# Attention and linear attention of a decoder block as small steps in an order fixed by the source

## The chip, the cores and the metric

The kernel runs as one program on one core of a Trainium2 chip. A core has a matrix engine (TensorE, PE), a vector engine (VectorE, DVE), an engine for activation functions (ScalarE, ACT), a general engine (GpSimd, POOL) and an engine that here only issues transfers (SyncE, SP). Each engine runs its own list of instructions in order and waits for the others by semaphores. The metric is the device time of one execution in microseconds (us). Each kernel is timed several times and the median counts; one execution is also taken apart by the hardware profiler.

## The reference

One decoder block over 512 tokens (T, in four blocks of P = 128) of width 1024. A mixer of two parallel parts, attention in a window of 128 with sinks and gated linear attention, is followed by a retrieval of 16 experts out of 16384 in each of 8 heads. A vector c scales, shifts and gates both (six modulations).

```python
h = rms_norm(x, norm1_w) * (1.0 + scale1) + shift1
proj = h @ w_in            # aq, ak, av, gq, gk, gv, gg, glr
scores = einsum('bnqhgd,bnkhd->bnhgqk', qb, kb) * 64 ** -0.5      # 8 heads, 2 of keys, width 64
probs = softmax(concatenate([where(mask, scores, -inf), sink], -1))[..., :-1]
att = einsum('bnhgqk,bnkhd->bnqhgd', probs, vb)

def step(state, inp):                                   # per head: 4 heads, keys 64, values 128
    b = cumsum(log_a); inter = (q * exp(b)) @ state
    decay = exp(b[t] - b[s])                            # for s <= t
    att = sum_d(q[t, d] * k[s, d] * decay[t, s, d]); intra = att @ v
    state = exp(b_last) * state + (k * exp(b_last - b)).T @ v
    return inter + intra
go = rms_norm(go, gla_norm_w) * silu(gg)
x = x + gate1 * (concatenate([att, go]) @ w_out)

h2 = rms_norm(x, norm2_w) * (1.0 + scale2) + shift2
x = x + gate2 * peer_ffn(h2, ...)                       # product keys, top 16, gather of u and v rows
return rms_norm(x, final_norm_w)
```

## The kernel before

**Precision.** Weights and activations are split into a high and a low part (`hi`, `lo`), and a product takes three matmuls: high by high, low by high, high by low (`mm3`, L78 to L80). The split is a copy on ScalarE and a subtraction on VectorE.

**Stages.** First come the norm, four modulations and the projections to q, k and the decays (up to L667). Then the stage that is changed, L677 to L892. Then the mixers (L907: the product of both parts with `w_out`, called `pw` in the trace, gate and second norm), the retrieval (first matmul `pq`) and the gathers and products of the experts, which take most of the time.

**The changed stage** has these works:
- `wide_part(g, ...)`: the projections to gv (g = 0) and gg (g = 1), 512 wide, in pairs of token blocks. Each pair takes two PSUM tiles `pn` and 8 steps of k with 6 matmuls. `wide_load(g)` brings `w_v` in two halves into the three `raw` tiles, and splits them.
- `attention(n)`, n = 0 to 3: for each half of the heads (jj) the mask and scores go into two banks `sc` (L723, L728), then maximum, Exp with sums (L739), Exp of the sink (L741), division by the sum (four scalings on VectorE, L745), transposes `pt` (L754), a copy `PT` (L755), the product with v into `po` (L760), and a copy into `mixA` (L763). Block 0 has one block of keys, the others two.
- `prep_*(1)` for the second 256 tokens: a scan of the decays, differences at NL levels, Abs (L332) and Exp (L335) over all levels in one pass each, products with q and k (the product q*k on GpSimd). The tile `Eg` holds them and is shared with gg.
- `gla_scores(n)`: decays by levels, 36 small matmuls and more into `pa` (a tile of two banks, `sc2`), the diagonal `pd` for two blocks each, merging under masks.
- `gla_state(n, gated)`: output `go` from state and scores (bank `po`), transposed keys `pk` and the new state's product `pS` (bank `pt`), four updates of the state S, then squares, root, and the scaling of `go`: for blocks 2 and 3 with gg in the same instruction, for 0 and 1 without; these get gg in `gla_gate`.
- `gla_gate(n)`: transposes `gt`, and the split of both parts for the mixers (`ah`, `al`, `gh`, `gl`).
- `mod_part(3)` and `(4)`: `w_ada` in four loads each through the same `raw` tiles, 8 sums on VectorE (L240), then 8 matmuls with one column (`mt`, L231).

**PSUM.** The eight banks are: `m` two (scores, `pd`, `mt`), `pt` one, `po` one, `sc2` two, `ph` two (`pn`, `gt`, later `pq`).

**The order.** Up to L667 the source fixes the order on each engine (`manual_schedule`). From L677 on, through the mixers, a planner orders the instructions by a simulated timeline:

```python
TCARGS = dict(schedule_with_timeline_sim=True)
```

Its input is the program text below; instructions that are ready early are moved ahead, on all engines and on SP's queue too. In the order that results, half of the 192 `pw` matmuls stand among the last steps of attention and of the states, and ScalarE's Silu of gg follows a load of its table.

```python
    gla_scores(0); attention(0); gla_scores(1)
    prep_scan(1); prep_diffs(1); prep_ends(1); prep_abs(1); prep_exp(1); prep_mults(1)
    wide_part(0, gv, (0, 1)); attention(1); wide_part(0, gv, (2, 3))
    gla_scores(2); gla_state(0, False); attention(2); gla_scores(3); gla_state(1, False)
    wide_part(1, gg, (0, 1)); attention(3); wide_part(1, gg, (2, 3))
    mod_part(3, ...); mod_part(4, ...)        # then Silu of gg, gg * gla_norm_w
    gla_state(2, True); gla_state(3, True)    # later gla_gate(0..3), mixers(0), mixers(2)
```

## Time and profile before

| | |
|---|---|
| three runs | 1457.5, 1461.05, 1461.68 us, median 1461.05 |
| profiled execution | 1457.49 us, of which the span is 1455.6 |
| TensorE busy | 1408.2 us, 97% |
| VectorE busy | 1274.2 us, 88% |
| ScalarE busy | 664.1 us, 46% |
| GpSimd busy | 611.8 us, 42% |
| transfers | 443.81 MB, 305 GB/s in the mean |

The span goes from the first instruction to the last; the profiled execution's own time is 1.9 us longer. Busy shares are means over stages with different limits: TensorE at 97% says that it is almost always at work, not that its work takes as little time as it could. The granted clock of TensorE tells how fast it was allowed to run. In a row of the timeline stand the start, the duration, the engine, the line, the operation, what it writes and reads, the shape and the number of instructions that were grouped; in brackets the idle time ahead and what ended it. A duration on TensorE is that of one matmul with its fill and drain; how much it costs in a stream is read from the distance between starts.

### The profile page before, as it was taken

The numbers are of one execution on the slowest core, as the hardware profiler recorded it, in microseconds if no ns is written. First come the engines' busy times: TensorE is split into PE (matmuls) and PEld (weight loads), VectorE is DVE, ScalarE is ACT, GpSimd is POOL, SyncE is SP. The second block draws the span as 40 slices with busy tenths as digits, with TensorE's granted clock in tenths as the row PEclk, the third lists the DMA queues.
The fourth block names the chain that finished last, engine by engine and source line by source line (L and its number), as shares of the span: only waits on it lengthen the run. The fifth ranks groups of instructions, "written<-read, shape, count | busy, mean of one in ns | idle before, by whom it ended". The sixth has DMA issues, their size and how long they took to land.

```text
span 1455.6 us, 23288 instructions
## 1 busy us (share of the span) xinstructions
PE 1408.2 (97%) x8788; PEld 1240.0 (85%) x8788; DVE 1274.2 (88%) x2338; ACT 664.1 (46%) x1108; POOL 611.8 (42%) x401
## 2 busy tenths in 40 slices
PE   6998989999999999999999999999999999999997
PEld 4776777798899999999998888888888888888885
DVE  7777746769999999999987999999999899899996
ACT  4555555643344467666774323333333323333333
POOL 2000000044443634423034776777777676555510
PEclk9998979999999999999999999999999999999999
DMA  9633407434256989989889999999999999999962
GB/s 355 243 124 115 169 6 254 152 133 182 95 179 254 415 308 360 362 316 345 306 307 407 413 412 412 413 412 409 397 403 396 401 372 412 399 411 411 412 251 73
DMA packets 129985, 443.81 MB, mean 305 GB/s; under 512 B 11952, under 2 KB 48592, under 8 KB 109520
## 3 DMA queue, kind: packets, MB, share of 16 engines
q1 hardware_dynamic: 71136, 256.40, 46.6%
q0 software_dynamic: 47136, 171.99, 30.1%
q10 hardware_dynamic: 11600, 13.93, 2.7%
q8 instruction: 69, 1.13, 0.3%
q14 instruction: 44, 0.36, 0.1%
HBM read 399.71 MB, written 42.47 MB: 304 GB/s over the span
## 4 chain that ended last, share of the span: by engine, by line
PE 77%; DVE 9%; issue 5%; DMA 4%; ACT 2%; POOL 2%; ACTq 0%; SPq 0%; POOLq 0%; DVEq 0%
PE acc L78 12%; PE acc L80 12%; PE acc L79 12%; PE ph L78 8%; PE ph L80 8%; PE ph L79 8%; POOL spr L1322 2%; PE pg L1243 2%; DMA wa<-in_w_ada_dram 2%; PE pw L78 1%; PE pw L79 1%; PE pw L80 1%; DVE macc L240 1%; PE pj L473 1%; PE pn L78 1%
## 5 line engine op out<-in xcount | busy, mean ns | idle before, releaser
L78 PE MATMUL ph<-h2Th,his 128*128 128x320 f32 x1024 | 320.1, 313 | 2.4 <-ACT his L1687 1.9
L80 PE MATMUL ph<-h2Th,los 128*128 128x320 f32 x1024 | 316.3, 310 | 2.5 <-DVE los L1694 1.8
L79 PE MATMUL ph<-h2Tl,his 128*128 128x320 f32 x1024 | 316.0, 309 | 0.0
L1378 POOL DMA_INDIRECT gu<-in_u_dram,ix_u x128 | 217.2, 1697 | 148.1 <-DVE gu L1388 82.9
L1413 POOL DMA_INDIRECT gv<-in_vP_dram,ix_v x128 | 210.8, 1647 | 109.6 <-DVE gacc L1418 86.9
L78 PEld LDWEIGHTS ph<-h2Th,his 128*128 128x128 f32 x1024 | 193.0, 188 | 4.3 <-ACT his L1687 2.1
L80 PEld LDWEIGHTS ph<-h2Th,los 128*128 128x128 f32 x1024 | 192.7, 188 | 3.3 <-DVE los L1694 2.0
L79 PEld LDWEIGHTS ph<-h2Tl,his 128*128 128x128 f32 x1024 | 193.1, 189 | 0.8
L1322 POOL DMA_INDIRECT spr<-in_u_dram,spix x64 | 104.8, 1637 | 170.5 <-DVE spr L1328 128.4
L79 PE MATMUL acc<-los,Ah 128*128 128x512 f32 x432 | 168.1, 389 | 0.0
L80 PE MATMUL acc<-his,Al 128*128 128x512 f32 x432 | 168.1, 389 | 0.0
L78 PE MATMUL acc<-his,Ah 128*128 128x512 f32 x432 | 168.0, 389 | 0.0
L1418 DVE SCALAR_TENSOR_TENSOR gacc<-gv,hg,gacc 128x1024 f32<-128x1024 f32 x127 | 162.6, 1281 | 1.6 <-DMA gv<-in_vP_dram,ix_v 1.4
L1388 DVE SCALAR_TENSOR_TENSOR gu<-gu,h2n 128x1024 f32<-128x1024 f32 x128 | 155.7, 1220 | 5.3 <-DMA gu<-in_u_dram,ix_u 5.3
L78 PE MATMUL acc<-hi,Ah 128*128 128x512 f32 x336 | 131.3, 391 | 0.0
L80 PE MATMUL acc<-hi,Al 128*128 128x512 f32 x336 | 131.1, 390 | 0.0
L79 PE MATMUL acc<-lo,Ah 128*128 128x512 f32 x336 | 130.7, 389 | 0.0
L1690 ACT ACTIVATE Ah<-gr 128x768 fp32r<-128x768 f32 x64 | 53.5, 836 | 135.8 <-PE acc L79 128.5
L71 ACT ACTIVATE his<-u 128x1024 fp32r<-128x1024 f32 x86 | 90.5, 1054 | 21.2 <-PE ph L79 9.5
L72 DVE TENSOR_TENSOR los<-u,his 128x1024 fp32r<-128x1024 f32 x75 | 91.6, 1224 | 8.4 <-ACT his L71 8.4
L80 PEld LDWEIGHTS acc<-his,Al 128*128 128x128 f32 x432 | 81.1, 188 | 16.9
L78 PEld LDWEIGHTS acc<-his,Ah 128*128 128x128 f32 x432 | 81.1, 188 | 16.8
(684 smaller groups left out, 2921.8 us busy)
## 6 DMA issues: line engine op xcount, KB each, us to landing
u<-in_uT_dram SPq DMA_DIRECT2D x43, 1024.0 KB, 7.6
gr<-Gd SPq DMA_DIRECT2D x15, 1536.0 KB, 11.1
Gd<-gs SPq DMA_DIRECT2D x10, 2048.0 KB, 9.8
gsp<-ge ACTq DMA_DIRECT2D x40, 320.0 KB, 6.1
wa<-in_w_ada_dram SPq DMA_DIRECT2D x12, 1024.0 KB, 5.4
wo<-in_w_out_dram SPq DMA_DIRECT2D x8, 1024.0 KB, 6.4
wq<-in_wq_dram SPq DMA_DIRECT2D x8, 1024.0 KB, 5.9
gp<-gsp SPq DMA_DIRECT2D x22, 320.0 KB, 10.7
```

Of the source, the lines that this page charges most:

```text
L71: nc.scalar.activation(hi, src, AF.Copy)
L72: lo_eng.tensor_tensor(lo, src, hi, OP.subtract)
L78: nc.tensor.matmul(acc, lh, rh, start=start, stop=False)
L79: nc.tensor.matmul(acc, lh, rl, start=False, stop=False)
L80: return nc.tensor.matmul(acc, ll, rh, start=False, stop=stop)
L1243: nc.tensor.matmul(pt[:, i, :], o12[:, g, 0, :, r], o2[:, g, m, :, r], start=(m == 0), stop=(m == 2))
L1322: nc.gpsimd.indirect_dma_start(out=sp[m], out_offset=None, in_=a["u"], in_offset=bass.IndirectOffsetOnAxis(ap=sp["ix", i][:, j:j + 1], axi ...
L1378: nc.gpsimd.indirect_dma_start(out=ur, out_offset=None, in_=a["u"], in_offset=bass.IndirectOffsetOnAxis(ap=ix_u[:, s:s + 1], axis=0))
L1388: nc.vector.scalar_tensor_tensor(ur, ur, 1.0, h2n, op0=OP.mult, op1=OP.mult, accum_out=hid[:, s:s + 1])
L1413: nc.gpsimd.indirect_dma_start(out=vr, out_offset=None, in_=a["vP"], in_offset=bass.IndirectOffsetOnAxis(ap=ix_v[:, s:s + 1], axis=0))
L1418: nc.vector.scalar_tensor_tensor(gacc, vr, hg[:, s:s + 1], gacc, op0=OP.mult, op1=OP.add)
L1690: nc.scalar.activation(grp(Ah), A, AF.Copy)
```

## The change

The stage from L677 to L892 is rewritten as generators, which yield before each small piece of work on one engine. A yield (`need`) names the engine, an assumed duration in us, the tiles that the piece takes, the marks that must have been set, and an urgency. `Weave.run` plays the threads against each other with one clock per engine: among the pieces of the engine that could start first, within 0.3 us of one another, it takes the one of highest urgency, and emits its instructions. The stage stands in `manual_schedule`, so the order of emission is the order on each engine. The mixers behind it are still ordered by the planner.

Further edits in the same stage:
- Attention's scores alternate between the two halves of the rows (s within j), after both masks. Of the four scalings by the sum, two stay on VectorE (L829), two go to ScalarE as a Copy with scale (L833).
- The preparation of the second 256 tokens: Abs (L1058) and Exp (L1060) in two parts, levels 0 to 3 and the rest; the products follow each part; q*k is on VectorE and not on GpSimd.
- `go` and `pk` with `pS` share one `sc2` tile, the kind that the scores `pa` use too, and hold it until the norm's products are written; `po` is left to attention, whose two halves are threads of their own, the second after the first's product. The products of the norm carry the weight `gnw`; gg is no longer multiplied by it, and `gla_gate` always multiplies by gg.
- Attention's scores are paced: unit u starts only after a row of `pn` that is given by `PACE` and `PACE0`.
- The first two halves of `w_v` are fetched in the stage ahead. The loads of `w_ada` stand between and behind those of `w_v`.
- Silu comes after all four `pn` of gg, and its table is loaded once, then the old one back. All of `gla_gate` and the split of attention's output stand in the stage, ahead of the mixers.

```diff
@@
+class Weave:
+    HOP, SLACK = 0.12, 0.3
...
+    def run(self, threads):
+        live = [[t, next(t), 0.0, urge, None] for urge, ts in threads for t in ts]
+        while live:
+            able = []
+            for th in live:
+                eng, us, take, after, urge = th[1]
+                if any(x not in self.marks for x in after) or any(len(self.slots[k]) < n for k, n in take.items()):
+                    continue
+                ready = [th[2] - self.HOP * (eng == th[4])] + [self.marks[x] for x in after] + [self.slots[k][n - 1] for k, n in take.items()]
+                able.append((max(self.busy.get(eng, 0.0), max(ready) + self.HOP), len(able), eng, th, th[3] + urge))
+            first = min(able)
+            at, _, _, th, _ = max((x for x in able if x[2] == first[2] and x[0] <= first[0] + self.SLACK),
+                               key=lambda x: (x[4], -x[1]))
...
@@
+    weave = Weave({"m": 2, "pt": 1, "po": 1, "sc2": 1, "ph": 2, "raw": 3, "hi": 3, "h32": 4, "sS": 2, "PT": 2, "sm": 2, "m4": 2})
...
+    def pace(u):
+        r = min(PACE * u - PACE0, 31)
+        return ([("sc", u - 1)] if u else []) + ([("rows", r // 16, r // 8 % 2 * 2, r % 8)] if r > 0 else [])
+
+    def attention(n, jj):
...
+        yield need("PE", 0.45 * w, {"m": 2, "sm": 1}, pace(2 * n + jj))
...
         for h in order[:2]:
             nc.vector.tensor_scalar(sS[:, h, :], sS[:, h, :], Z[:, h:h + 1], None, op0=OP.mult)
+        mark(("Z", n, jj))
+        yield need("ACT", 0.4 + 0.42 * w)
+        for h in order[2:]:
+            nc.scalar.activation(sS[:, h, :], sS[:, h, :], AF.Copy, scale=Z[:, h:h + 1])
...
-    def gla_state(n, gated):
+    def gla_state(n):
...
-        go = bank(f"go{n}", "po")
+        two = bank2(f"go{n}")
+        go, pk = two[:, 0], two[:, 1]
...
-                nc.vector.tensor_scalar(gv[n][:, gsl], go[:, gsl], r4[:, h:h + 1], None, op0=OP.mult)
+            nc.vector.scalar_tensor_tensor(gv[n][:, gsl], go[:, gsl], y[:, h:h + 1], gnw, op0=OP.mult, op1=OP.mult)
+        two = go = pk = None
+        free("sc2")
...
+    def second_exps():
+        yield need("ACT", 0.5, {}, ["b1", ("Dpe", 0)])
+        nc.scalar.activation(Eg[:, NL + 1, :], preps["b"], AF.Exp, scale=1.0 / TAU)
+        mark("e1")
+        for L0, L1 in ((0, 4), (4, NL + 1)):
+            yield need("ACT", 1.8 if L0 == 0 else 1.4, {}, [("diff", L1 - 1)])
+            nc.scalar.activation(Eg[:, L0:min(L1, NL), :], Eg[:, L0:min(L1, NL), :], AF.Abs)
+            yield need("ACT", 1.8)
+            nc.scalar.activation(Eg[:, L0:L1, :], Eg[:, L0:L1, :], AF.Exp, scale=-1.0 / TAU)
+            mark(("E", L1 - 1))
...
+        weave.run([(2.0, [gla_scores(0, ([], [])), gla_scores(1, ([], []))]), (1.9, [wide_load(0), wide_load(1)]),
+                   (1.4, [gla_gate(n) for n in range(NT)]), (1.3, [gla_state(n) for n in range(NT)]),
+                   (1.2, [attention(n, jj) for n in range(NT) for jj in range(2)]),
+                   (1.1, [second_exps(), second_prep(), gla_scores(2, ready), gla_scores(3, ready)]),
+                   (1.0, [wide_all(0, gv)]), (0.8, [wide_all(1, gg, [("Spe", 2), ("Spe", 3)]), gates()]),
+                   (0.0, [modulation(3, [("w", 1, 7)]), modulation(4)]),
+                   (0.0, [attention_parts(n) for n in range(NT)])])
```

The order moves at many places; three show how. **TensorE, the scores of attention.** Before, one mask and the two products of one half of the rows (`sc`) stood between `pn` matmuls:

```order
L784 MATMUL pa_1301<-Eg 64x32 x6
L350 MATMUL pd_1355<-sel,Eg 128x2 x4
L723 LDWEIGHTS identb
L723 MATMUL sc_1412<-am,identb 128x512
L728 MATMUL sc_1412<-kT,qT 128x256 x2
L79 MATMUL pn_1645<-wv102l,hTh 128x512
```

After, both masks come first, and the products alternate, with steps of other heads between them:

```order
L798 LDWEIGHTS identb
L798 MATMUL sc_1285<-am,identb 128x512
L798 LDWEIGHTS identb
L798 MATMUL sc_1286<-am,identb 128x512
L859 MATMUL po_1259<-PT_1279,vN 64x128 x4
L804 MATMUL sc_1285<-kT,qT 128x256
L804 MATMUL sc_1286<-kT,qT 128x256
L842 MATMUL pt_1302<-ident,sS_1253 128x128 x4
L804 MATMUL sc_1285<-kT,qT 128x256
L804 MATMUL sc_1286<-kT,qT 128x256
```

The four products of a unit, which some units of before had already side by side, now always alternate between the two banks.

**ScalarE, around the second preparation.** Before, Abs (L332) and Exp (L335) took all their levels at once, with the evictions of `pn` (L708) between them and attention's copy `PT` (L755) behind:

```order
L741 ACTIVATE es_942<-es_942 128x4
L332 ACTIVATE Eg<-Eg 128x3584
L798 ACTIVATE at_175<-atc_179 64x4x64 x2
L708 ACTIVATE gv_109<-pn_1093 128x512
L708 ACTIVATE gv_110<-pn_1094 128x512
L335 ACTIVATE Eg<-Eg 128x4096
L755 ACTIVATE PT_959<-pt_960 128x512
```

After, the two parts of each (L1058, L1060) stand between single steps, and the new scalings (L833) are among these:

```order
L833 ACTIVATE sS_1079<-sS_1079,Z_1063 128x128 x2
L1058 ACTIVATE Eg<-Eg 128x2048
L848 ACTIVATE PT_1120<-pt_1106 128x512
L1060 ACTIVATE Eg<-Eg 128x2048
L867 ACTIVATE mixA_114<-po_1050 128x512
L774 ACTIVATE gv_109<-pn_897 128x512
L774 ACTIVATE gv_110<-pn_898 128x512
```

The copy `PT` and the evictions thus stand ahead of the second part, and not behind the whole.

**TensorE, the end of the stage.** Before, the last steps of attention and of the states lay among the `pw` matmuls of the mixers:

```order
L80 MATMUL pw_2072<-his,gl_2032 128x512
L760 MATMUL po_1696<-PT_1777,vN 64x128 x4
L754 MATMUL pt_1789<-ident,sS_1748 128x128 x4
L760 MATMUL po_1696<-PT_1788,vN 64x128 x4
L814 MATMUL pk_1925<-ident,kl_1046 128x128 x2
L809 MATMUL go_1916<-S_170,qe_1047 128x128
```

After, the last `pn` is followed by the sums over partitions (`mt`) and two transposes (`gt`), and then come all `pw`:

```order
L122 MATMUL pn_1813<-wv17h,hTl 128x512
L1080 MATMUL mt_1970<-ones,macc_1636 128x1 x8
L1080 MATMUL mt_1982<-ones,macc_999 128x1 x8
L990 MATMUL gt_1996<-ident,gv_109 128x128 x4
L990 MATMUL gt_2006<-ident,gv_110 128x128 x4
L120 MATMUL pw_2068<-his,ah_1290 128x512
```

All 192 `pw` matmuls of the mixers now lie behind the states.

## The prediction

> **What bounds the kernel now.** I read the page first, then the busy time of two stretches, then TensorE's rows in order of time through them, and last the rows of the engines that it waits for.

> ```profile
> span 1455.6 us, 23288 instructions
> PE   6998989999999999999999999999999999999997
> PEclk9998979999999999999999999999999999999999
> PE 77%; DVE 9%; issue 5%; DMA 4%; ACT 2%; POOL 2%; ACTq 0%; SPq 0%; POOLq 0%; DVEq 0%
> ```

> TensorE (PE) carries 77% of the chain that ended last, and after its start it is at 8 and its clock below 9 in two slices only, the fourth and the sixth. A slice is 36.4 us: these are 109 to 146 and 182 to 218 us, and both lie in the changed part. The two orders of TensorE agree up to the first `pn` matmul at 99.26 us and again from the first matmul of the retrieval stage (`pq`) at 274.38 us; on the other engines the last difference lies in the same stage. So what decides is the time between those two matmuls, 175.1 us now; all that comes later has the same order and shifts with it.

> ```profile
> 99.20:213.70 114.50, 104.55 (x798) 78.96 (x799) 75.20 (x194) 57.00 (x146) 1.34 (x1) 0.88 0.30 103
> 213.70:274.40 60.70, 58.73 (x309) 46.53 (x308) 46.23 (x91) 37.66 (x78) 0.00 (x0) 0.98 0.56 192
> ```

> Columns: stretch, its us, busy PE, PE weight loads, DVE, ACT, POOL, granted clock, DMA share, GB/s. In the first stretch VectorE is busy 66% and ScalarE 50%, and TensorE has 10 us idle and 12% of its clock missing. Its own rows show that the two belong together:

> ```profile
> 102.37 0.39 PE L78 MATMUL pn<-wv000h,hTh 128*128 128x512 f32 x1
> 102.60 0.39 PE L79 MATMUL pn<-wv000l,hTh 128*128 128x512 f32 x1
> ...
> 115.34 0.48 PE L754 MATMUL pt<-ident,sS 128*128 128x128 f32 x1 [3.26 <-DVE sS L745]
> ...
> 121.67 0.63 PE L79 MATMUL pn<-wv00l,hTh 128*128 128x512 f32 x1
> 122.10 0.63 PE L80 MATMUL pn<-wv00h,hTl 128*128 128x512 f32 x1
> ...
> 124.17 0.39 PE L79 MATMUL pn<-wv01l,hTh 128*128 128x512 f32 x1
> ...
> 130.87 0.79 PE L78 MATMUL pn<-wv000h,hTh 128*128 128x512 f32 x1 [2.66 <-ACT gv L708]
> ...
> 134.39 0.39 PE L80 MATMUL pn<-wv002h,hTl 128*128 128x512 f32 x1
> ...
> 199.27 1.12 PE L760 MATMUL po<-PT,vN 128*64 128x128 f32 x8 [3.44 <-ACT PT L755]
> ...
> 212.98 1.11 PE L754 MATMUL pt<-ident,sS 128*128 128x128 f32 x4 [0.59 <-DVE S L825]
> ...
> 216.25 0.39 PE L80 MATMUL pw<-his,al 128*128 128x512 f32 x1
> ...
> 231.08 0.66 PE L760 MATMUL po<-PT,vN 128*64 128x128 f32 x8 [0.75 <-ACT PT L755]
> ...
> 263.26 0.50 PE L78 MATMUL pw<-his,ah 128*128 128x512 f32 x1 [0.75 <-DVE mg L928]
> ```

> Three waits of 3.26, 2.66 and 3.44 us; after each, matmuls start 0.43 us apart and not 0.23, until 124.2, 134.4 and 216.2: 8.8, 3.5 and 17.0 us at half rate, of which 14.6 us are lost. With the shorter waits (0.59, 0.75, 0.75, and 0.33 in a row below) 11.8 us are idle. After the two of 0.75 the rate stays full: the `po` group at 231.08 takes 0.66 and not 1.12.

> **The work that stays.** The start-to-start times at full rate:

> ```profile
> 152.96 0.66 PE L754 MATMUL pt<-ident,sS 128*128 128x128 f32 x4
> 153.54 1.25 PE L784 MATMUL pa<-Eg 64*64 64x32 f32 x72
> 154.73 0.66 PE L760 MATMUL po<-PT,vN 128*64 128x128 f32 x8
> ...
> 156.27 1.05 PE L350 MATMUL pd<-sel,Eg 128*128 128x2 f32 x8
> 157.18 0.38 PE L723 MATMUL sc<-am,identb 128*128 128x512 bf16 x1
> 157.49 1.13 PE L728 MATMUL sc<-kT,qT 64*128 64x256 f32 x4
> 158.54 0.50 PE L79 MATMUL pn<-wv102l,hTh 128*128 128x512 f32 x1
> 158.88 0.40 PE L80 MATMUL pn<-wv102h,hTl 128*128 128x512 f32 x1
> ...
> 191.02 1.13 PE L728 MATMUL sc<-kT,qT 64*128 64x256 f32 x8
> 192.08 0.50 PE L79 MATMUL pn<-wv10l,hTh 128*128 128x512 f32 x1
> ...
> 232.43 0.49 PE L809 MATMUL go<-S,qe 128*128 128x128 f32 x2 [0.33 <-ACT mixA L763]
> ...
> 234.24 0.47 PE L78 MATMUL pw<-his,ah 128*128 128x512 f32 x1
> ...
> 368.10 1.84 PE L231 MATMUL mt<-ones,macc 128*128 128x1 f32 x16
> 369.81 0.48 PE L80 MATMUL pq<-h2Th,los 128*128 128x512 f32 x1
> ```

> (Most fp32 matmuls are recorded twice.) `pn`: 192 by 0.228 = 43.7. `pt` and `po`: 14 groups each by 0.58 = 16.2. Three `pa` still to come, 48 small matmuls each at 1.19/36 us, and 0.4 for four larger ones ahead (an estimate: as 12 small ones): 5.9; one `pd` 0.9. Scores `sc`: six units of two masks (0.31) and a paired group (1.06) 10.1; the two of block 0, half as wide, 2.1. `go` 1.8 three times, 0.9 once; `pk` and `pS`, three each, 2.9 (as `pt`, by their count); `mt` two by 1.71 = 3.4; four `gt` 1.8. Then 192 `pw` 43.7 and four `x2t` groups 2.3. Together 139.3. Each return to `pn` or `pw` starts 0.34 and not 0.23 apart, and I take as much for leaving: 0.2 a visit. The order shows 22 visits now (4.4) and 34 afterwards (6.8).

> Now: 139.3 + 4.4 + 11.8 idle + 14.6 clock + 2.1 for unpaired scores = 172.2, against 175.1: 2.9 us stay unplaced and are taken over as they are. The unpaired scores are in those rows: two matmuls of one half of the rows take 1.05 (157.49 to 158.54), four of alternating halves 1.06 (191.02); four units of now lose 0.53 each, and all new units alternate: **2.1 less**; more visits: **2.4 more**.

> **The waits of the new order.** The three long waits go: the work for `pt` (3.26) was behind sums that waited for a load; the eviction (2.66) and `PT` (3.44) behind long work of ScalarE.

> ```profile
> 112.07 2.60 DVE L240 SCALAR_TENSOR_TENSOR macc<-wa,scs,macc 128x1024 f32<-128x1024 f32 x2 [4.00 <-DMA wa<-in_w_ada_dram]
> ...
> 126.27 3.19 ACT L332 ACTIVATE Eg<-Eg 128x3584 f32<-128x3584 f32 x1 [6.93 <-DVE Eg L317]
> ...
> 131.33 3.62 ACT L335 ACTIVATE Eg<-Eg 128x4096 f32<-128x4096 f32 x1
> ...
> 194.86 1.28 ACT L884 ACT_TABLE_LOAD   x1
> 196.16 1.15 ACT L884 ACTIVATE Eg<-Eg 128x512 f32<-128x512 f32 x2
> ...
> 252.95 0.71 ACT L953 ACTIVATE xs<-x,rb0y 128x512 f32<-128x512 f32 x1
> ...
> L745 DVE TENSOR_SCALAR sS<-sS,Z 128x256 f32<-128x256 f32 x24 | 6.9, 351 | 0.3
> ```

> The sums (L240) now stand one or two at a time behind other work, and their loads alternate with those of w_v on SP: each waits there for one of three tiles, and behind it all later loads. The tightest, the second half of w_v's second group, waits for the second sum (some 136 us) and is wanted near 148. Both long passes are cut in two: at 3.19/3584 us a column, 1.8 and 1.4 us. I set the new order along with these durations: where PE reaches a row before its input, that is a wait. I find 0.7 before the second score unit (its two banks free only when the first unit's exponentials end), 1.3 before the second pair of `pn` (evicted behind an Exp part), 1.3 before `po` of block 1 (`PT` behind an Exp part), 0.8 before the second `pn` group, some four of 0.4 at the state steps; at the end, where four Silu follow the last `pn` and the first 1.05 us `his` follows them, 0.6 before `gt` and 2.1 before `pw`. With 2.3 for the mixers' own (three like 263.26), 10.7 against 11.8 now: **1.1 less**. Nothing missed would make this about 3; every joint 0.2 later (60 joints, of which I count half as uncovered) 6 more.

> **Clock: 14.6 now.** None of these waits is as long as the shortest that halved the rate (2.66); up to 0.75 the rows show no loss; between, none. The last one follows `mt`, which streams a single column, so the array does little for 7 us: 0 to 4.2 (half of the 8.8 us above), I take 2 for that, nearer the short intervals: **12.6 less**.

> [...]

> **Normalisation.** Of 32 scalings 16 leave VectorE (0.35 or 0.28 each, 5 us) for ScalarE, where the nearest row (0.71 for twice the width) bounds one by 0.36 and 0.71, I take 0.4: 6.4 us. ScalarE's 57 us become some 72 in 108 (the last attention block's copies come ahead of the mixers too); VectorE keeps some 79, since the product that GpSimd did and two more gate products come, and four weightings go. Both lie beside TensorE's 98 us of this part and cost 0 while they keep up; without cover 6.4. The weight of the norm is now multiplied in with the root, by the same four instructions.

> **Loads behind the weave.** The x loads wait for tiles that the last `mt` frees (some 204 us), and the fourth w_out load stands behind them: 3.1 MB, at the 192 GB/s of the second stretch 16 us, at full share (192/0.56) 9. It is wanted after 72 `pw` (16.4 us from 207.5) less 2.3 for its two halves, at 221.6: 1.6 us to spare at the slow end, cost 0.

> **Sum:** 2.1 − 2.4 + 1.1 + 12.6 = 13.4 less, with the Silu table loaded once instead of twice (1.28 and its return, on ScalarE, which the 3.44 us wait held) already in the waits. Say 13: 1457.5 → 1444.5 for the profiled execution; the runs' median is 1461.05, so **1448**.

> **Rivals.** *Short waits that keep the clock low.* Some 60 joints pass through 8 banks; if waits of 0.4 to 1.3 us, close together, kept the rate at half as long as now (29 us), the 14.6 return and it stays at 1461. [...] Against it: at 231.08 and 232.43 two waits lie 1.4 us apart, and the rate was full behind them (0.66, 0.49). For it: three of them in 3 us are in no row here. 10%.

> *One tile for scores and states (slower).* `go` leaves its own bank and takes the tile of the scores, held until the norm is written, so the next state cannot start before: `go`, squares, root, refinement and four products, about 8 us by their rows, with only 7.6 us of TensorE's rows between the first two. If sums ahead on VectorE make each of three hand-overs 2.9 us long, the rate halves too: 3 × (2.9 + 4.9) = 23 more, 10 slower: 1471. It decides from about 1.7 hand-overs of that size. For it: strict order on three engines at 67 to 73%. Against: 12 to 13 us of rows lie between the later states. 8%.

> *Mixers without cover.* Now 96 of 192 `pw` fill the last states; then all follow, with VectorE needing some 44 us in 50 (46 in 60.7 now), and x loads wait on the released tiles ahead of the fourth w_out load. VectorE at 80% takes 55: 5 less gain, 1453. 10%.

> *All waits gone:* 8 better, 1440 and below: 7%.

> **Numbers.** 65% for the forecast with its own range 1440 to 1456. What a measurement can tell is 0.3%, 4.4 us. Faster 65 + 10 + 7 = 82%, within 10%, slower 8%. The range, 1436 to 1460, takes in the waits without misses and the return of the clock's loss.

> **What would show it.** Right: the first `pq` at 259 to 264 us, no PE wait above 2.5 us from 99 us, clock at 0.95 and above there; the first `pw` at 206 to 212. Wrong: windows below 0.9 with waits all under 1.5 (first rival), `go` waiting for the norm's product (second), DVE above 95% after the first `pw` (third). A later order that does not shift by the same amount would break the step from the stage to the time.

## The result and the profile after

| | before | after |
|---|---|---|
| median of four runs each | 1460.63 us (1457.5 to 1461.68) | 1439.83 us (1437.5 to 1442.22) |
| ratio, 95% interval | | 0.9861 [0.9837, 0.9885] |
| profiled execution | 1457.49 us | 1442.22 us |
| first `pn` to first `pq` | 175.12 us | 159.74 us |

The change makes the kernel 1.4% faster, some 20 us. The profiled execution of before was the fastest of its runs and that of after the slowest of its own, so the two traces show 15.3 of the 20 us. What the other 5 were is seen below, in a second profile of the same kernel.

The page of after: the two weak slices of TensorE are gone, and the chain of work that ended last has much the same shares (before: PE 77%, DVE 9%).

```profile
span 1440.4 us, 23298 instructions
PE   5999999999999999999989999999999999999997
PEclk9999999999999999999999999999999999999999
PE 75%; DVE 10%; issue 6%; ACT 3%; DMA 3%; POOL 2%; SPq 0%; ACTq 0%; POOLq 0%; DVEq 0%
```

The first `pn` starts at 98.57, the first `pq` at 258.31 us. Behind it lie 1440.4 − 258.3 = 1182.1 us, before 1455.6 − 274.4 = 1181.2: all of the gain is in the stage, and what follows has only shifted. TensorE's waits in that stretch, by the view of waits (engine, line, what it waited for; us in total, times, longest):

```profile
PE x2t L1177 <- ACT xs L1173: 2.0, 1, 2.0
PE pa L891 <- issue: 2.0, 1, 2.0
PE pn L120 <- ACT gv L774: 1.4, 1, 1.4
PE pw L120 <- DVE mg L1148: 0.8, 2, 0.4
PE po L859 <- ACT PT L848: 0.7, 1, 0.7
```

With three more of 0.6 and less they make 7.9 us, where before had 11.8. The long ones of before (3.4 for `PT`, 3.3 for the scaled scores, 2.7 for the eviction) are gone. Two of 2.0 are new: one for `xs` in the mixers, and one for `pa` that the trace puts down to nothing ("issue"). Both have a stretch at half rate behind them, and so has the end of the stage (columns: stretch, its us, busy PE, PE weight loads, DVE, ACT, POOL, granted clock, DMA share, GB/s):

```profile
105.00:113.00 8.00, 6.57 (x25) 4.64 (x25) 7.26 (x22) 3.54 (x15) 0.00 (x0) 0.57 0.15 33
201.00:209.00 8.00, 7.83 (x31) 6.57 (x31) 7.00 (x8) 6.67 (x10) 0.00 (x0) 0.57 0.18 42
243.00:251.00 8.00, 6.52 (x25) 5.20 (x26) 6.64 (x13) 6.07 (x14) 0.00 (x0) 0.79 0.44 154
```

0.43 of 8 us is 3.4 us lost, twice, and 0.21 of 8 us 1.7: 8.5 us. The same reading of before:

```profile
113.00:125.00 12.00, 9.66 (x110) 7.74 (x111) 9.88 (x25) 2.09 (x10) 0.00 (x0) 0.57 0.28 91
130.00:135.00 5.00, 4.13 (x11) 3.32 (x12) 3.45 (x8) 4.95 (x5) 0.00 (x0) 0.66 0.37 106
199.00:217.00 18.00, 17.14 (x79) 15.19 (x80) 8.21 (x20) 9.84 (x28) 0.00 (x0) 0.53 0.01 1
```

5.2, 1.7 and 8.5: 15.4 us, of which a part lies in the idle time itself.

### The profile page after: what moved, and what is told of

Its sections match the earlier page's. It is cut to its first block, busy times and chain, and to the rows that moved or that the text cites. A ratio compares the mean times of both kernels' runs of the same rounds, so it can differ in the third digit from the quotient of the medians.

```text
span 1440.4 us, 23298 instructions
## 1 busy us (share of the span) xinstructions
PE 1396.3 (97%) x8788; PEld 1229.5 (85%) x8788; DVE 1272.8 (88%) x2321; ACT 669.0 (46%) x1124; POOL 611.7 (42%) x400
## 3 DMA queue, kind: packets, MB, share of 16 engines
q8 instruction: 69, 1.13, 0.3%
## 4 chain that ended last, share of the span: by engine, by line
PE 75%; DVE 10%; issue 6%; ACT 3%; DMA 3%; POOL 2%; SPq 0%; ACTq 0%; POOLq 0%; DVEq 0%
PE acc L122 12%; PE acc L120 12%; PE acc L121 12%; PE ph L122 8%; PE ph L120 8%; PE ph L121 8%; POOL spr L1542 2%; PE pg L1463 2%; PE pw L121 1%; PE pw L120 1%; PE pn L120 1%; DVE macc L282 1%; PE pw L122 1%; DMA u<-in_uT_dram 1%; PE pj L120 1%
## 5 line engine op out<-in xcount | busy, mean ns | idle before, releaser
L121 PEld LDWEIGHTS acc<-los,Ah 128*128 128x128 f32 x432 | 81.1, 188 | 16.9
L120 PEld LDWEIGHTS acc<-his,Ah 128*128 128x128 f32 x432 | 81.1, 188 | 16.9
```

Source lines behind the costliest of these rows:

```text
L120: nc.tensor.matmul(acc, lh, rh, start=start, stop=False)
L121: nc.tensor.matmul(acc, lh, rl, start=False, stop=False)
```

## The experiments

My theory was that of the prediction: the order takes away the three long waits, and with them the stretches at half rate. Against it stood that the edits do it (two parts of Abs and Exp, ScalarE's share of the scalings, alternating scores), whatever the order; and for the clock, that something other than waits holds it low. Each group of four runs had its own runs of the kernel before beside it, and ratios are to those. A span and a stretch are of the one profiled execution; a time is the median of several.

### The change again, as a measure

The kernel is unaltered.

> The change itself, unaltered, as the measure for the three beside it: 1437 to 1443. If the 1.96 us at 106.43 us, for which the trace names no cause, belongs to the program, it is there again with about 5 us at half rate behind it; if it is chance, this profile lacks it and its span is some 4 us shorter.

1439.02 us, ratio 0.9868 [0.9848, 0.9888]. This profile has no wait at `pa`, and a span of 1436.4 us, 4.0 less than the first. So the 1.96 us and the 6.8 us at half rate behind them belong to one execution and not to the program, and this second profile is the one to set against before. First `pn` 99.61, first `pq` 254.68: 155.07 us, **20.05 less than before**, which is the difference of the medians, 20.8, but for 0.7. Its waits:

```profile
PE x2t L1177 <- ACT xs L1173: 2.0, 1, 2.0
PE pn L120 <- ACT gv L774: 1.8, 2, 1.4
PE sc L798 <- ACT sS L820: 0.9, 2, 0.4
PE pw L120 <- DVE mg L1148: 0.8, 2, 0.4
...
PE pw L121 <- DVE los L114: 0.5, 1, 0.5
```

and its clock:

```profile
104.00:112.00 8.00, 7.14 (x135) 5.25 (x132) 7.26 (x22) 5.58 (x19) 0.00 (x0) 1.00 0.17 69
199.00:208.00 9.00, 8.47 (x33) 6.29 (x33) 8.13 (x10) 6.08 (x9) 0.00 (x0) 0.62 0.35 104
241.00:249.00 8.00, 6.56 (x32) 5.36 (x33) 6.63 (x13) 6.06 (x14) 0.00 (x0) 1.00 0.39 144
```

Only the end of the stage costs clock here, 0.38 × 9 = 3.4 us. The wait of 2.0 us for `xs`, which cost 1.7 us of clock in the first profile, is there again and costs none; the last section shows what differed.

### The new pieces, ordered by the planner

```diff
-    with tc.manual_schedule(engines={mybir.EngineType.PE, mybir.EngineType.Activation, mybir.EngineType.DVE,
-                                     mybir.EngineType.SP, mybir.EngineType.Pool}):
+    if True:
...
```

(The load of the old table keeps its place in program order. The planner's input is the pieces in the order in which `Weave` emits them.)

> The new pieces, tiles and edits, but the order of the stage left to the planner again. If the fixed order itself carries the gain (the planner puts long work of ScalarE or sums of VectorE ahead of what TensorE waits for, as before), two or three waits of TensorE above 2.5 us come back with half-rate stretches behind them, and the time is 1452 to 1462. If the edits carry it (two parts, half the scalings on ScalarE, alternating scores), no such wait is there and the time is 1438 to 1446.

1460.64 us, ratio 1.0002 [0.9985, 1.0020]. **All of the gain is gone.** TensorE is idle for 13.0 us in the stage, and 13.7 us of clock are lost. The waits are back, at other places:

```profile
PE sc L798 <- ACT sS L820: 4.7, 2, 3.7
PE pw L120 <- DVE mg L1147: 2.6, 1, 2.6
PE x2t L1176 <- DVE xs L1174: 2.5, 1, 2.5
PE pt L842 <- DVE sS L829: 2.1, 1, 2.1
```

The longest, 3.7 us, is of the kind of before. VectorE's rows ahead of it:

```profile
106.02 2.61 DVE L282 SCALAR_TENSOR_TENSOR macc<-wa,scs,macc 128x1024 f32<-128x1024 f32 x2 [1.92 <-DMA wa<-in_w_ada_dram]
108.55 0.42 DVE L813 TENSOR_REDUCE mx<-sc 128x2 f32<-128x256 f32 x1
```

The maximum of the scores stands behind two modulation sums that waited for their load. The planner put them there again, with all edits in place. So under the planner the edits together are worth nothing that can be measured, and the gain needs the fixed order. Whether the order gives all of it without the edits is not shown: further below three edits are taken back one at a time under a fixed order, but the tile shared by states and scores, the later Silu, and q*k on VectorE never are.

### Before, with Abs and Exp in two parts

```diff
...
-    prep_abs(1)
-    prep_exp(1)
+    prep_abs(1, 0, 4)
+    prep_exp(1, 0, 4)
+    prep_abs(1, 4, NL)
+    prep_exp(1, 4, NL + 1)
```

> The kernel before, with one edit alone: Abs and Exp of the second preparation in two parts, order by the planner. If the length of these passes made two of the three long waits (2.66 and 3.44 us, with 3.5 and 17.0 us at half rate behind them), up to 6.1 us idle and 10.2 us of clock go: 1445 to 1452. If the planner's order made them, the time stays within 1456 to 1464.

1460.46 us, ratio 1.0003 [0.9990, 1.0015]: nothing. The planner leaves the four parts in one row on ScalarE, with the evictions behind all of them:

```profile
122.15 1.91 ACT L332 ACTIVATE Eg<-Eg 128x2048 f32<-128x2048 f32 x1 [2.54 <-DVE Eg L317]
124.10 1.92 ACT L335 ACTIVATE Eg<-Eg 128x2048 f32<-128x2048 f32 x1
126.28 1.49 ACT L332 ACTIVATE Eg<-Eg 128x1536 f32<-128x1536 f32 x1 [0.26 <-DVE Eg L317]
127.79 1.91 ACT L335 ACTIVATE Eg<-Eg 128x2048 f32<-128x2048 f32 x1
129.61 1.07 ACT L708 ACTIVATE gv<-pn 128x512 f32<-128x512 f32 x2
```

7.2 us of work stand ahead of the eviction, whole or in parts. The wait for the eviction is shorter for it, 1.81 us. The 3.45 us wait for `PT` is there as well: the long passes were not its cause, and the expectation above was wrong to count it. In before, `PT` at 198.62 us stands right behind 3.7 us of other work on ScalarE, from 194.86: the load of Silu's table, two Silu, and the load of the old table back.

### The change, with Abs and Exp in one part

```diff
-        for L0, L1 in ((0, 4), (4, NL + 1)):
+        for L0, L1 in ((0, NL + 1),):
...
```

(The assumed durations are set to 3.2 and 3.6 us, and the products wait for all levels.)

> The change, with Abs and Exp in one part each (3.2 and 3.6 us on ScalarE), order fixed by the source, which is worked out anew for these lengths. If the two parts are needed, evictions or PT stand behind 3.6 us once or twice: one or two waits above 2 us with 2.5 us or more of clock lost behind each, 1444 to 1450. If an order that knows the lengths can go around them: 1437 to 1443.

1437.97 us, ratio 0.9849 [0.9827, 0.9870]: no slower than the change. In its profile TensorE's waits ahead of the mixers are all below 0.6 us, though ScalarE is held twice for more than 3 us:

```profile
122.76 3.23 ACT L1058 ACTIVATE Eg<-Eg 128x3584 f32<-128x3584 f32 x1
130.76 3.66 ACT L1060 ACTIVATE Eg<-Eg 128x4096 f32<-128x4096 f32 x1
```

An order that reckons with their length puts them where TensorE has work that does not need ScalarE. The split in two is not needed either way.

### The change, with all scalings on VectorE

```diff
-        for h in order[:2]:
+        for h in order:
             nc.vector.tensor_scalar(sS[:, h, :], sS[:, h, :], Z[:, h:h + 1], None, op0=OP.mult)
-        yield need("ACT", 0.4 + 0.42 * w)
-        for h in order[2:]:
-            nc.scalar.activation(sS[:, h, :], sS[:, h, :], AF.Copy, scale=Z[:, h:h + 1])
```

(VectorE's assumed duration grows by as much.)

> The change, with all scalings by the sum on VectorE. 16 scalings of 0.28 or 0.35 us, 5 us, go back to VectorE, which was busy 85 of 107 us in the stage. If TensorE's rows cover it: 1437 to 1443, no difference to the change. If VectorE sets the pace where it is full (9.5 of 10 us at 130 to 140 and 160 to 170): 5 to 6.4 us more, 1445 to 1447.

1443.53 us, ratio 0.9885 [0.9864, 0.9906]. It lies between the two expectations, 0.2% above the change by the ratios, with intervals that overlap, so the runs alone do not tell it from the change; the trace shows more. From the first `pn` (100.22) to the first `pq` (258.63) it takes 158.4 us, 3.3 more than the repeated change. TensorE waits 2.91 us for VectorE's `atc`, at 154.79 us, and 1.68 us for its `gv` ahead of `gt`. VectorE's rows up to the first of these leave almost no gap:

```profile
150.16 1.28 DVE L813 TENSOR_REDUCE mx<-sc 128x2 f32<-128x512 f32 x2
...
152.43 2.22 DVE L913 COPY_PREDICATED atc<-lm,pa 128x128 f32<-128x128 uint16 x6
154.68 0.45 DVE L916 COPY_PREDICATED atc<-lm,pd 128x256 f32<-128x256 uint16 x1
```

So with this order the scalings hold up VectorE, and half of them on ScalarE are worth about 3 us in the trace, of which 1.7 are one more stretch at half rate (at 183.3 us, shown in the last section).

### Wider `mt`, in the change and before

```diff
-            nc.tensor.matmul(pb[:, i:i + 1], acc[:, i * P:(i + 1) * P], ones[:, 0:1], start=True, stop=True)
+            nc.tensor.matmul(pb[:, i * 64:i * 64 + 64], acc[:, i * P:(i + 1) * P], ones[:, 0:64], start=True, stop=True)
...
```

(What is read afterwards is one column in 64.)

> The change, with one edit that leaves the order as it is: the 16 matmuls of mt stream 64 columns of ones instead of one (of which one is used). If what halves the clock at the end of the stage is that one-column matmuls keep the array nearly empty, the 3.4 us lost at 199 to 209 us go for the most part, less 0.3 for the longer matmuls: 3 faster than the change beside it. If it is the waits and joints around them: no difference, within 1.

> The kernel before, with the same edit; the order is the same up to these matmuls. There the 3.44 us wait at 199 us was followed by 17 us at half rate, with mt in the midst (200.8 to 206.6 and 211.4). If the wait alone set this stretch, as the prediction has it, it stays near 17 us and the time at 1458 to 1463. If mt kept it low, it ends after 4 to 9 us, and the time is 1453 to 1457.

In the change: 1439.12 us, no difference to the 1439.02 beside it. Before: 1459.37 us, ratio 0.9998 [0.9983, 1.0012], no difference. The clock did move in the profiles. In the change (first row) the end of the stage lost 0.21 × 8 = 1.7 us and not 3.4, in before (second row) the stretch from 199 us lost 0.43 × 12 = 5.2 and not 8.5:

```profile
200.00:208.00 8.00, 6.71 (x27) 4.91 (x26) 7.16 (x9) 5.18 (x8) 0.00 (x0) 0.79 0.38 114
```

```profile
199.00:211.00 12.00, 11.02 (x62) 10.45 (x62) 2.85 (x9) 4.91 (x17) 0.00 (x0) 0.57 0.01 1
```

In before, the planner's order is the same up to `mt` and differs a little behind it; TensorE reached its later rows sooner and waited there: 0.94 us for the state's `S`, 0.53 for `los`, 1.51 for `mg`, where before had 0.59, none and 0.75. The stage is 1.1 us shorter (99.91 to 273.88), too little for the runs to tell. So the one-column matmuls seem to share in keeping the clock low. For before that is one execution against one. In the change the four profiles with this order and one-column `mt` at the end (the first, its repetition, other banks, scores by halves) all lost 3.4 us there, the one with 64 columns 1.7. It then lost another 1.7 us behind the wait for `xs`, where the repetition lost none, so its stage is no shorter (156.3 us). The times show no difference, and 1.7 us would lie within their intervals.

### Spreading `mt`

```diff
-        yield need("PE", 1.8, {"m": 1})
-        pb = bank(f"mt{v}")
         for i in range(KD):
+            yield need("PE", 0.22, {"m": 1} if i == 0 else {}, (), 3.0)
+            if i == 0:
+                pb = bank(f"mt{v}")
             nc.tensor.matmul(pb[:, i:i + 1], acc[:, i * P:(i + 1) * P], ones[:, 0:1], start=True, stop=True)
+            yield need(f"gap{v}", 0.6)
```

> The change, with the 16 matmuls of mt put one by one between the last pn, so that no stretch of 3.5 us streams single columns. If this stretch halves the clock at the end of the stage, the clock stays full from 195 us to the first pw and 3.4 us go: 1435 to 1436, and the first pq comes 3 us earlier than in the repeated run of the change. If the waits and transposes ahead of pw do it, the clock falls there all the same: 1438 to 1440.

1445.44 us, ratio 0.9904 [0.9889, 0.9919]: slower than the change, and neither expectation. The rows of ScalarE, TensorE and VectorE behind the last `pn` show the main reason:

```profile
199.00 1.30 ACT L774 ACTIVATE Eg<-pn 128x512 f32<-128x512 f32 x2 [2.63 <-PE pn L122]
199.27 0.40 PE L122 MATMUL pn<-wv17h,hTl 128*128 128x512 f32 x1
200.32 1.28 ACT L1095 ACT_TABLE_LOAD   x1
201.61 1.67 ACT L1095 ACTIVATE Eg<-Eg 128x512 f32<-128x512 f32 x3
202.27 1.89 DVE L986 TENSOR_TENSOR gv<-gv,Eg 128x512 f32<-128x512 f32 x3 [5.18 <-ACT Eg L1095]
203.02 1.26 PE L990 MATMUL gt<-ident,gv 128*128 128x128 f32 x8 [3.36 <-DVE gv L986]
```

Eviction, table load, Silu and gate product take some 3.4 us before the first `gt` can start. In the repeated change `mt` lay exactly over them: the last `pn` starts at 195.80 us, and `gt` at 199.55 without a wait.

```profile
196.03 3.63 PE L1080 MATMUL mt<-ones,macc 128*128 128x1 f32 x32
```

Moved away, the matmuls of `mt` leave 3.36 us idle, and a stretch of 3.4 us at half rate follows that wait too, so the clock is no better (3.4 us lost in all, as in the repetition). The stage is 160.3 us, 5.2 more, of which 4.6 are idle time. `mt` had covered that chain.

### Spreading `mt`, with one part, and `xs` on VectorE

The two edits shown above together, and then, on top:

```diff
-            if half:
-                nc.scalar.activation(xs, x1[:, 512:], AF.Copy, scale=r)
-            else:
-                nc.vector.tensor_scalar(xs, x1[:, :512], r, None, op0=OP.mult)
+            nc.vector.tensor_scalar(xs, x1[:, half * 512:half * 512 + 512], r, None, op0=OP.mult)
```

> The change with Abs and Exp in one part each (which alone took 1438.0) and mt one by one between the last pn. If both effects are there and add up: 1434 to 1436. If the order that is worked out anew brings other waits: 1438 to 1441.

> The one before in this list, with both halves of the second norm's scaled rows (xs) written by VectorE; ScalarE wrote the second. At 242 us x2t waited 2.0 us for ScalarE's xs, which stood behind the split of w_out. If that order on ScalarE made the wait, it goes, with 0 to 2.5 us of clock: 2 to 4 faster than the one before. If the root of the norm is late, x2t waits for VectorE's xs as long: no difference, within 1.

1445.27 us, ratio 0.9906 [0.9890, 0.9921], and 1442.15 us, ratio 0.9882 [0.9865, 0.9899]. The first has the same 3.36 us ahead of `gt`, and what one part gave is not seen beside it. In the second the 2.02 us wait for `xs` is gone, and 0.58 and 1.05 us at the same place have come instead. The 3 us between the two speak for ScalarE's order having made a part of that wait, but the intervals touch, and the two profiles differ the other way (158.4 and 160.1 us from `pn` to `pq`, with three stretches of 3.4 us at half rate in the second and two in the first). It stays open.

### Other banks for `pw`

```diff
-            pw = [bank(f"pw{n}{q}") for n in pair]
+            pw = [bank(f"pw{n}{q}", ("m", ("pt", "po")[i])[q]) for i, n in enumerate(pair)]
```

> The change, with the second half of the columns of each pw pair in the banks that attention has released (pt, po), where both halves shared two banks. At 241 to 249 us TensorE had nothing to do until VectorE's mg released a bank: 2.0 and 0.4 us idle, 0.6 at a wait in the line, 5 us at half rate behind it. If the shared banks make this: 4 to 5 faster than the change beside it. If the second norm does (xs and its root, which every x2t needs): no more than 1.

1439.71 us, ratio 0.9862 [0.9842, 0.9883], against 0.9868 beside it: no difference. The waits for `mg` went, but `x2t` waited 0.58 and 1.16 us for the two halves of `xs` all the same, and `pw` 0.27 us behind it. So it is the second norm that TensorE waits for here, more than the banks.

### Scores by halves

```diff
-        for j in range(2):
+        for s in range(2):
             yield need("PE", 0.98 * w)
-            for s in range(2):
+            for j in range(2):
```

> The change, with the four score products of a unit ordered by halves of the rows and not alternating; every other instruction stands where it stood. By the size in the prediction (0.53 us for a unit of blocks 1 to 3, half of that for block 0) this costs 6 x 0.53 + 2 x 0.27 = 3.7 us: 1442 to 1443. By the distances between starts in the traces (two products of one half 1.05, four that alternate 1.06, so 1.04 for a unit, and 0.63 for one of block 0) it costs 6 x 1.04 + 2 x 0.63 = 7.5 us: 1446 to 1447.

1443.16 us, ratio 0.9891 [0.9874, 0.9908], 0.2% above the change, with overlapping intervals; by the profile the stage is 157.14 us, 2.1 more. Both sizes were wrong, and the rows show where they fail:

```profile
115.16 1.13 PE L804 MATMUL sc<-kT,qT 64*128 64x256 f32 x4
116.22 0.66 PE L842 MATMUL pt<-ident,sS 128*128 128x128 f32 x4
116.80 1.13 PE L804 MATMUL sc<-kT,qT 64*128 64x256 f32 x4
...
125.11 1.14 PE L804 MATMUL sc<-kT,qT 64*128 64x256 f32 x8
```

Two products of one half with other work behind them take 1.06 us (115.16 to 116.22). All four in a row (125.11) take 1.07 to the next row's start, at 126.18, as well, though they no longer alternate: it was enough that the two halves followed each other. In the repeated change the same place has two alternating pairs around the same `pt`, at 0.63 each:

```profile
115.16 0.70 PE L804 MATMUL sc<-kT,qT 64*128 64x256 f32 x4
115.79 0.66 PE L842 MATMUL pt<-ident,sS 128*128 128x128 f32 x4
116.38 0.70 PE L804 MATMUL sc<-kT,qT 64*128 64x256 f32 x4
```

Only two of the eight units were interrupted, and so only these lost, 0.43 us on each of four pairs, 1.7 us in all. The single records of the row at 125.11 start in four pairs, 0.013 us apart (125.111 and 125.124 the first, 125.431 and 125.444 the second), as those of an alternating row in the repeated change do (124.730 and 124.737): two ran side by side here too. How that comes about when both products of one half stand first in the order, no run here shows.

## Why the prediction was right

1439.83 us lies inside the range of 1436 to 1460, 8 us below the forecast of 1448 and just below the range of the likeliest case. First `pw` and first `pq` came at 204.2 and 258.3 us, and in the repeated change at 201.3 and 254.7, a little ahead of the 206 to 212 and 259 to 264 that were set; no wait of TensorE was above 2.02 us, the clock was 0.95 and 0.98 in the mean of the stage, and the later order did shift as one.

The stage's time splits into three: idle time of TensorE, work (distances between starts, less idle time, halved where the granted clock stood at half), and the rest, which is what the clock cost. Before: 11.8 + 149.3 + 14.0 = 175.1. The repeated change: 7.4 + 144.7 + 3.0 = 155.1.

| step of the prediction | predicted | measured |
|---|---|---|
| clock | −12.6 | −11.0 |
| waits | −1.1 | −4.4 |
| unpaired scores | −2.1 | −4.7 (16.9 to 12.2 us) |
| more visits (`pn`, `pw`) | +2.4 | +2.8 (91.7 to 94.5 us) |
| decay products `pa` | 0 | −1.4 (7.5 to 6.0 us) |
| other work of TensorE | 0 | −1.3 |
| sum | −13.4 | −20.0 |

**The mechanism** holds. The long waits went, the clock came back, and both needed the order, as the planner's run shows. The chain had the right place: what lies behind the first `pq` took 1181 to 1182 us in all three profiles. The sizes hold less well: the sum is two thirds of what was measured, and the terms that it missed by most are the waits and the scores.

**Clock.** Close in sum, in part by luck, and the rule behind it was wrong. In the first profile, which lost 8.5 us where the repetition lost 3.4, this term would be about −6. I took each stretch as set by the length of the wait ahead of it, with 2.66 us as the shortest that counts. But a wait of 2.91 us cost nothing in one run and one of 1.81 us cost 1.7 in another; of eight profiles with a wait of 2.0 us for `xs`, two lost nothing and six 1.7 us; and with wider `mt` the 17 us of before were 10.2, behind the same 3.45 us wait. The end of the stage cost 3.4 us, where I took 2 out of 0 to 4.2.

**Waits** were mis-sized: 10.7 expected, 7.4 found. Where I set 2.1 us ahead of `pw`, 0.5 stood; where I set 1.3 twice for an Exp part ahead of evictions and `PT`, 0.5 and 0.5. The four state steps of 0.4 came to 0.9 in all. Nothing ahead of `gt` (0.6 expected), since `mt` covers it. The one I had not seen, 2.0 us for `xs`, is in the mixers. The loads behind the stage cost nothing, as reckoned: no wait of TensorE there is put down to a transfer.

**Scores** were mis-sized by more than half, from rows that I quoted. Two lone products of a half cost 1.05, and so a unit of two such pairs loses 1.05, not 0.53 (in two of the four units both pairs stood alone); and block 0's two units, whose halves also stood apart at 0.64 a pair, I left out.

**Visits** came out right. The small `pa` matmuls I had taken as kept: 15 groups in before, 8 in the repeated change, and fewer interruptions of small work were worth 1.4 us.

**The normalisation** at no cost was right; the price without it was 3.3 us in the trace, for 6.4 named.

**The rivals.** Short waits that keep the clock low: no. In the repeated change two of 0.4 lie 0.7 us apart and others of 0.5 and 1.4 follow, and the clock stands at 1.00 there. One tile for scores and states: `go` waited 0.2 and 0.6 us, never near 2.9. Mixers without cover: in part; from the first `pw` to the first `pq` it is 53.4 us for the 50 reckoned, with 3.3 us of waits. All waits gone: no, yet the time falls at that rival's 1440, by way of work and not of waits. A rival that I had not listed is that some named parts carry nothing. It holds for the two parts of Abs and Exp, and for all edits together without the order.

## What to carry to other kernels

When a planner by a simulated timeline orders a stage, look ahead of TensorE's long waits for work that it put in front: here sums that waited for a load, long passes, a table load. Cutting the passes in two did not help, as the planner stacked the pieces again, while an order that reckons with their lengths could take even the long ones. Before moving work off the end of a stage, look what chain runs beside it: 3.5 us of `mt` covered 3.4 us of eviction, table load and Silu, and moving it cost more than the clock that it was meant to save. And one profile of each kernel can be off by several us: here one wait without a known cause, with its half rate, made the first profile of after 4 us longer than the second.

## What the runs showed of the hardware

**Half rate came in units.** What the clock cost between 99 and 275 us was 1.7 us or a whole multiple of it in every profile: 15.4 before (nine), 8.5 after (five), 3.4 in its repetition (two), 13.7 with the planner's order (eight), 11.9 before with wider `mt` (seven). One unit is 3.4 us at half rate (in the clock records of the traces 3.413). In the planner's run, two units follow 3.73 us of waiting (first fence). In the change with all scalings on VectorE (second fence) none follows the longest wait, 2.91 us ahead of 154.79, and one follows the first `mt`, which had no wait ahead or within:

```profile
109.00:118.00 9.00, 6.73 (x20) 4.99 (x20) 6.54 (x13) 6.22 (x13) 0.00 (x0) 0.62 0.35 117
```

```profile
150.00:160.00 10.00, 7.04 (x66) 5.21 (x60) 9.58 (x27) 5.84 (x18) 0.00 (x0) 1.00 0.47 143
181.60:183.30 1.70, 1.70 (x17) 1.69 (x16) 1.59 (x7) 1.54 (x7) 0.00 (x0) 1.00 0.27 28
183.30:187.30 4.00, 4.00 (x15) 3.19 (x14) 3.60 (x17) 2.23 (x11) 0.00 (x0) 0.57 0.74 250
```

One and the same wait cost a unit in one execution and nothing in another: the 2.0 us for `xs` cost 1.7 us in the first profile of the change and none in its repetition. Nor was it long waits alone that had a unit behind them: in before with two parts one followed 1.81 us of waiting (0.28 × 6 = 1.7 us lost at 129 to 135 us), and the one in the second fence followed 1.7 us of one-column matmuls with no wait at all.

**A wait without a known cause.** The 1.96 us ahead of the last `pa` at 106.43 us, in one of the profiles of the change and in none of its repetitions, has no releaser in the trace. Its cause stays open.
